# Keys, queries and values of dilated attention groups projected in class order: a strided stationary operand in a two-layer mixer on one core

## The chip, the core and the metric

The kernel runs on one core of a Trainium2 chip. The metric is device time in microseconds (us). TensorE (PE in the profile, its weight loads PEld), VectorE (DVE), ScalarE (ACT) and GpSimd (POOL) run in parallel, each with its own instruction stream; SyncE (SP) issues most DMAs.

## The reference, cut to what matters

Two decoder layers over 512 tokens and 1024 features. In each layer one normed input is projected for four attention branches, A to D. Branch B has three groups of 8 heads; group 0 attends to neighbouring tokens, group 1 to every 4th, group 2 to every 16th.

```python
B_GROUPS = ((128, 1), (512, 4), (2048, 16))      # window, dilation
xn = rms_norm(x, norm_gain[l])
qbm = rms_norm(b_q.reshape(shp_b), qk_gain_b[l, 0])
kbm = rms_norm(b_k.reshape(shp_b), qk_gain_b[l, 1])
yb = dilated_mixture(qbm, kbm, b_v.reshape(shp_b), rel_bias)
...
def to_sub(t):    # keys and queries of one residue class stand together
    t = t.reshape(b, sub_len, dil, h, dh).transpose(0, 2, 1, 3, 4).reshape(b * dil, sub_len, h, dh)
```

## The kernel before

The normed residual is held feature-major, `xhl` [128 partitions, 2 parts, 8 row tiles, 512 tokens], as two exact fp32r parts (high and low). Every product of two such operands takes three passes: high by high, high by low, low by high. A weight slot is loaded by an SP DMA (`next_slot`, L402), its high part is made on ACT (L405) and its low part on DVE (L411); six split slots are kept.

A job `("pair", branch, p, g)` projects q, k and v of two heads: 384 columns, four slots. `t_bank` fills one PSUM bank per tile of 128 tokens: the stationary operand is the residual (128 tokens), the moving one the weights, 8 row tiles by 3 passes = 24 matmuls (L512 to L514). `f_bank` is the other orientation: weights stationary, all 512 tokens moving, 24 matmuls (L536 to L538). There are four such accumulating banks (`acc`).

Groups 1 and 2 of branch B (`perm` in `do_pair`) need their tokens in class order: token 4i + c at place 128c + i. So 4 pairs of heads x 2 groups x 2 layers = 16 jobs are permuted. For these, before the change: the four calls of `t_bank` make q and k alone (256 columns) in natural order; after the norms (`norm_qk`: square, sum, power, gain, split over ACT, DVE and POOL), PE transposes each head to feature-major (L676, L689) and the ACT copies out of PSUM (`q_out` L680, `k_out` L693) write with a permuting pattern; the unpermuted jobs use L682 and L696 instead. v is made by `f_bank`, copied by ACT in class order (L734), transposed back on PE in four 128x128 pieces (L737), and split into its two parts by one ACT and one DVE instruction of 512 columns (`split_ps`, L547, L548). For other jobs v lies in columns 256 to 384 of each `t_bank` and is split out of it, 128 columns at a time. `k_swap` copies k with high and low exchanged by four POOL DMAs (L701, L702). Attention of a class (`attend`, L971 to L1026) and the copy back to natural order (`o_sum`, L1041) take class order as input in both versions.

Each engine's instruction order is made by a scheduler from the list `PLAN`: earlier pieces are preferred, later ones (gates z, the merges of finished branches, the next pair) fill in where they are ready. It also places the tiles in SBUF.

Of the kernel before, what the change touches and what calls it, by code (L numbers as in the profile page):

```python
# [82 lines left out]
def job_slots(job):  # L83
    """Per weight slot: a list of (source, rows of 128, columns)."""
    kind = job[0]
    if kind in ("idx", "cin", "pair", "d0", "d1"):
        c = chunk_cols(job)
        return [[("w_in", 2 * i + j, c) for j in range(2)] for i in range(4)]
    if kind == "z":
        c = Z_OFF[job[1]] + job[2] * 128 + np.arange(128)  # L90
        return [[("w_in", 4 * i + j, c) for j in range(4)] for i in range(2)]
    if kind == "merge":
        n, ft = job[1], job[2]
        c = OFF_G + n * D + ft * 128 + np.arange(128)
        f = ft * 128 + np.arange(128)
        return [[("w_in", j, c) for j in range(6)],
                [("w_in", j, c) for j in (6, 7)] + [(("w_branch", n), j, f) for j in range(4)]]
    if kind == "out":
        f = job[1] * 128 + np.arange(128)
        return [[("w_out", 4 * i + j, f) for j in range(4)] for i in range(2)]  # L100
    if kind == "cq":
        q = job[1] * 384 + np.arange(384)
        return [[("w_q_b", 0, q), ("w_q_b", 1, q)]]
    if kind == "ckv":
        p = job[1]
        h = np.arange(64)
        kv = np.concatenate([(2 * p) * 128 + h, (2 * p + 1) * 128 + h,
                             (2 * p) * 128 + 64 + h, (2 * p + 1) * 128 + 64 + h])
        return [[("w_kv_b", 0, kv)]]
    raise ValueError(kind)  # L110


def plan():
    """The order of a layer's work; what comes first is preferred where several pieces are ready."""
# [127 lines left out]
def build(ctx, tc, A, depth=2, dump=None):  # L242
# [97 lines left out]
    def make_skew(seg, r):  # L340
        """Rows r and r + 1 of a segment, 128 copies each, so that a load can shift copy i by i."""
        r0, nr = (C_ROW, 1) if seg == "C" else (SEG_ROWS[seg][0] + r, 2)
        o = SEG_A if seg == "C" else seg
        w = SEG_W[o]
        d = dp.tile([nr, 128, w], F32, name=f"skew{seg}_{r}")
        g = gdram[r0:r0 + nr, o:o + w]
        sy.dma_start(d, bass.AP(tensor=g.tensor, offset=g.offset, ap=[[SEG_LEN, nr], [0, 128], [1, w]]))
        for i in range(nr):
            skew[seg, r0 + i] = (d[i], w)
# [9 lines left out]
    def next_skew():  # L359
        """The next segment's copies, behind the weights requested so far."""  # L360
        if skews:
            with tc.issue_after(wdma[0].ins):
                make_skew(*skews.pop(0))

    def load_bias(row, seg, n):
        """[128, n] tile whose row i is the segment's row shifted by i to the right."""
        while (seg, row) not in skew:
            next_skew()
        b = T([128, 512], F32, "bias")[:, :n]
        g, w = skew[seg, row]  # L370
        with tc.issue_after(wdma[0].ins):
            sy.dma_start(b, bass.AP(tensor=g.tensor, offset=g.offset + 127, ap=[[w - 1, 128], [1, n]]))
        return b

    def rsqrt(eng, r, ss, n, scale, eps=EPS):
        """r = 1 / sqrt(ss * scale + eps) on [128, n]."""
# [5 lines left out]
    def layer(l, xt):  # L382
# [32 lines left out]
        def gain_parts():  # L415
            """x * gain as hi and lo per row tile: the first products need not wait for the norm."""
# [87 lines left out]
        def t_bank(slots, w, t, c0=0, c1=None, x=None):  # L504
            c1 = w if c1 is None else c1
# [3 lines left out]
            for kt in range(KT):  # L509
                h, lo = slots[kt // 2]  # L510
                a = (kt % 2) * w
                mm(o[:, :c1 - c0], x[kt][:, 0, ts], h[:, a + c0:a + c1], start=kt == 0, stop=False)  # L512
                mm(o[:, :c1 - c0], x[kt][:, 0, ts], lo[:, a + c0:a + c1], start=False, stop=False)  # L513
                mm(o[:, :c1 - c0], x[kt][:, 1, ts], h[:, a + c0:a + c1], start=False, stop=kt == KT - 1)  # L514
            return o

        def t_banks(slots, w, x):
            """Banks of all token tiles, filled together; x: hi and lo per row tile."""
# [12 lines left out]
        def f_bank(parts, mh, ml, w=S):  # L531
            """parts: (hi, lo) stationary views [128, 128] per row tile; moving operands mh, ml: [128, w] each."""
# [11 lines left out]
        def split_ps(hi, lo, src, scale=None):  # L544
            """hi + lo = src (* scale), src in PSUM."""
# [92 lines left out]
        def evac(o, n, scale=1.0):  # L638
            """A copy of a bank's first n columns, so that the bank is free before the norms are known."""
# [7 lines left out]
        def norm_qk(o, t, x, gi, scale=1.0):  # L647
            """o: two heads of q and of k in PSUM; hi and lo of the normed ones to x[:, t], [128, 4, 2, 64]."""
# [13 lines left out]

        def perm_view(x, perm):
            return x.rearrange("p (c i) -> p i c", c=4) if perm else x
# [4 lines left out]
        def q_out(uq, qx, hf, h0, n, perm):  # L669
            """Heads of qx [128, 2, n, 2, 64] (half hf of the tokens) to uq[:, h0:h0 + n], feature-major."""  # L670
            for i0 in range(0, n, 2):
# [6 lines left out]
                if perm:  # L678
                    dst = uq[:, h0 + i0:h0 + i0 + m].rearrange("p h (c i) -> p h i c", c=4)[:, :, hf * 64:hf * 64 + 64]
                    ac.copy(dst, src.rearrange("p h (i c) -> p h i c", c=4))  # L680
                else:
                    ac.copy(uq[:, h0 + i0:h0 + i0 + m, hf * 256:hf * 256 + 256], src)  # L682

        def k_out(kk, x, hf, perm):
            """The two k heads of x (half hf of the tokens), hi on top of lo, to kk(h, 0)."""
# [4 lines left out]
            for i in range(2):  # L690
                src = p[:, i * 256:(i + 1) * 256]
                if perm:
                    ac.copy(kk(i, 0).rearrange("p (c i) -> p i c", c=4)[:, hf * 64:hf * 64 + 64],  # L693
                            src.rearrange("p (i c) -> p i c", c=4))
                else:
                    ac.copy(kk(i, 0)[:, hf * 256:hf * 256 + 256], src)  # L696

        def k_swap(kk):
            """kk(h, 1): lo on top of hi."""
# [8 lines left out]
        def do_pair(job):  # L708
# [6 lines left out]
            for t in range(NT):  # L715
                if t % 2 == 0:
                    x = T([128, 2, 4, 2, 64], F32R, "qk")
                o = t_bank(slots, 384, t, 0, 256 if perm else 384)
                if not perm:
                    v = o[:, 256:384].rearrange("p (h d) -> p h d", h=2)  # L720
                    split_ps(vv[:, t, :, 0:64], vv[:, t, :, 64:128], v)
# [3 lines left out]
                if t % 2:  # L725
                    q_out(uq, x, t // 2, 0, 2, perm)
                    k_out(kk, x, t // 2, perm)
            k_swap(kk)
            if perm:
                o = f_bank([(slots[k // 2][0][:, (k % 2) * 384 + 256:(k % 2) * 384 + 384],  # L730
                             slots[k // 2][1][:, (k % 2) * 384 + 256:(k % 2) * 384 + 384]) for k in range(KT)],
                           xhs, xls)
                vp = T([128, 512], F32, "tmp")
                ac.copy(perm_view(vp, True), nat_view(o, True))  # L734
                p = ps_t()
                for t in range(NT):
                    pe.transpose(p[:, t * 128:(t + 1) * 128], vp[:, t * 128:(t + 1) * 128], idf)  # L737
                pv = p.rearrange("p (t h d) -> p t h d", t=NT, h=2)
                split_ps(vv[:, :, :, 0:64], vv[:, :, :, 64:128], pv)
            return uq, ks, vv  # L740

        def do_d():
# [4 lines left out]
            for t in range(NT):  # L747
# [7 lines left out]
                if t % 2:  # L755
                    q_out(uqs[0], x, t // 2, 0, 2, False)
                    k_out(kk, x, t // 2, False)
# [3 lines left out]
            for t in range(NT):  # L761
# [10 lines left out]
                for i in range(3):  # L772
# [5 lines left out]
                    if t % 2:  # L778
                        q_out(uqs[i + 1], qxs[i], t // 2, 0, 2, False)
# [3 lines left out]
        def do_cin():  # L783
# [23 lines left out]
            # rotary key, shared by the heads  # L807
# [24 lines left out]
        def do_cq(p, cT):  # L832
            """The normed and rotated queries of two pairs, [128, 2, 4, 96] per half of the tokens."""
# [73 lines left out]
        def scores(kind, step, qk, bias, nm, den, mask, sink, both):  # L907
            """exp of the scores less their maximum, sums to den, minus the maximum to nm."""
# [52 lines left out]
        def attend(kind, qk, v, bias, nm, den, norm, both, mask=None, sink=None):  # L961
            """qk(qb, k0, n): (lhsT, rhs) of the passes; v(kb): stationary [128, 128]; nm/den [128, NT] columns.
            Returns the O bank: rows of V's high part on top of rows of its low part."""
# [73 lines left out]
        def o_sum(dst, o, h, perm):  # L1037
            """Add the halves of an O bank into rows h*64.. of dst, in token order."""
# [290 lines left out]
```

## Time and profile before

| | us |
|---|---|
| median of 3 runs | 1953.87 |
| lowest, highest | 1952.23, 1957.49 |
| the profiled execution: its span, first to last instruction | 1949.2 |
| PE busy in it | 1884.5 (97%) |
| DVE busy | 1331.1 (68%) |
| ACT busy | 1103.0 (57%) |
| POOL busy | 728.5 (37%) |
| granted TensorE clock, mean | 0.986 of full |

For the profiled execution the profile gives the span; the median lies 4.7 us above it. "Busy" of PE counts overlapping matmul records once; how fast PE works is read from the distance between the starts of consecutive matmuls, not from their durations, since a matmul's record overlaps the next one's. PEld is PE's loading of a stationary operand, which runs beside the matmul of the one before it.

### The profile page before, as it was taken

How to read it: one execution, taken by the hardware profiler on the slowest of the kernel's cores; microseconds unless marked ns; L12 is line 12 of the kernel's file. 1: busy time of each engine (PE TensorE's matmuls, PEld its weight loads, DVE VectorE, ACT ScalarE, POOL GpSimd, SP SyncE). 2: the span in 40 equal slices, each digit the busy share in tenths (PEclk: the TensorE clock that was granted, in tenths of full speed). 3: DMA queues.
4: the chain of work that ended last, by engine and by line, in shares of the span. 5: the costliest groups of instructions: out<-in, count | busy, mean ns of one | idle time of the engine just before them, and what ended most of it. 6: DMA issues, size and time to landing. Idle time of an engine off the chain costs nothing.

```text
span 1949.2 us, 33221 instructions
## 1 busy us (share of the span) xinstructions
PE 1884.5 (97%) x11348; PEld 1695.6 (87%) x11348; DVE 1331.1 (68%) x3410; ACT 1103.0 (57%) x2650; POOL 728.5 (37%) x1186
## 2 busy tenths in 40 slices
PE   8759999999989999999999999999999999999999
PEld 7648889989878998998889988899899989898887
DVE  7649777758476866665469888676768686766542
ACT  6538666656455565554347776566555656555431
POOL 3615353424233346640005345253343343755000
PEclk9879999999989999999999999999999999999999
DMA  4223233342334243332252222233333333333233
GB/s 163 84 91 95 67 90 103 105 113 88 110 105 118 80 121 105 99 98 82 91 187 85 82 66 93 74 88 83 94 105 113 101 101 91 117 96 101 80 92 108
DMA packets 103420, 193.47 MB, mean 99 GB/s; under 512 B 21510, under 2 KB 35924, under 8 KB 103252
## 3 DMA queue, kind: packets, MB, share of 16 engines
q1 hardware_dynamic: 92372, 173.52, 29.4%
q0 software_dynamic: 10880, 17.83, 4.2%
q8 instruction: 90, 1.47, 0.3%
q14 instruction: 78, 0.64, 0.1%
HBM read 168.84 MB, written 12.83 MB: 93 GB/s over the span
## 4 chain that ended last, share of the span: by engine, by line
PE 88%; DMA 4%; DVE 2%; ACT 2%; POOL 2%; issue 1%; SPq 1%; DVEq 0%; ACTq 0%; POOLq 0%
PE acc L537 14%; PE acc L536 14%; PE acc L538 14%; PE acc L512 9%; PE acc L513 9%; PE acc L514 9%; PE S L923 4%; PE T L994 3%; PE T L1014 2%; DMA cbuf<-wall 1%; DMA sd<-st 1%; PE T L1033 1%; PE T L1026 1%; PE T L676 1%; PE T L689 1%
## 5 line engine op out<-in xcount | busy, mean ns | idle before, releaser
L411 DVE TENSOR_TENSOR cbufr<-cbuf,cbufr 128x768 fp32r<-128x768 f32 (+3 forms) x396 | 357.6, 906 | 140.5 <-ACT cbufr L405 139.0
L405 ACT CAST cbufr<-cbuf 128x768 fp32r<-128x768 f32 (+3 forms) x396 | 304.9, 774 | 262.4 <-PE acc L537 195.9
L513 PE MATMUL acc<-cbufr 128*128 128x384 f32 (+1 forms) x1152 | 365.8, 318 | 0.0
L512 PE MATMUL acc<-cbufr 128*128 128x384 f32 (+1 forms) x1152 | 364.1, 317 | 0.0
L514 PE MATMUL acc<-cbufr 128*128 128x384 f32 (+1 forms) x1152 | 363.9, 316 | 0.0
L536 PE MATMUL acc<-cbufr 128*128 128x512 f32 x896 | 354.5, 396 | 0.9 <-ACT raw L642 0.9
L538 PE MATMUL acc<-cbufr 128*128 128x512 f32 x896 | 353.9, 395 | 0.0
L537 PE MATMUL acc<-cbufr 128*128 128x512 f32 x896 | 353.6, 395 | 0.0
L513 PEld LDWEIGHTS acc<-cbufr 128*128 128x128 f32 x1152 | 218.7, 190 | 3.0 <-issue 1.1
L512 PEld LDWEIGHTS acc<-cbufr 128*128 128x128 f32 x1152 | 218.5, 190 | 2.7 <-ACT U L696 0.7
L514 PEld LDWEIGHTS acc<-cbufr 128*128 128x128 f32 x1152 | 218.7, 190 | 2.3 <-issue 0.8
L379 POOL TENSOR_TENSOR nr<-nx,cbuf 128x4 f32<-128x4 f32 (+2 forms) x200 | 211.6, 1060 | 11.1
L538 PEld LDWEIGHTS acc<-cbufr 128*128 128x128 f32 x896 | 168.9, 188 | 34.0
L536 PEld LDWEIGHTS acc<-cbufr 128*128 128x128 f32 x896 | 169.0, 189 | 32.7 <-ACT raw L642 1.3
L537 PEld LDWEIGHTS acc<-cbufr 128*128 128x128 f32 x896 | 169.1, 189 | 32.3 <-issue 0.7
L958 POOL TENSOR_SCALAR P<-P,rd 128x128 f32<-128x128 f32 x192 | 117.3, 621 | 195.4 <-DVE rd L956 136.2
L378 POOL TENSOR_SCALAR nx<-nss 128x4 f32<-128x4 f32 (+2 forms) x200 | 62.3, 311 | 272.2 <-DVE nss L653 243.1
L701 POOL DMA_DIRECT2D U<-U x68 | 39.3, 578 | 311.4 <-ACT U L693 190.4
L547 ACT CAST PT<-T 128x128 fp32r<-128x128 f32 (+2 forms) x224 | 102.9, 478 | 64.0 <-PE T L994 38.0
L548 DVE TENSOR_TENSOR PT<-T,PT 128x128 fp32r<-128x128 f32 (+2 forms) x224 | 119.8, 548 | 22.0 <-ACT PT L547 20.3
L945 ACT ACTIVATE P<-P,nm 128x128 f32<-128x128 f32 x192 | 101.9, 533 | 57.4 <-DVE nm L942 56.7
L642 ACT COPY raw<-acc 128x256 f32<-128x256 f32 (+2 forms) x192 | 70.4, 377 | 107.9 <-PE acc L514 74.9
(256 smaller groups left out, 3954.0 us busy)
## 6 DMA issues: line engine op xcount, KB each, us to landing
cbuf<-wall SPq DMA_DIRECT2D x284, 384.0 KB
cbuf<-wall SPq DMA_DIRECT2D x96, 256.0 KB
U<-U POOLq DMA_DIRECT2D x136, 128.0 KB, 2.8
bias<-skew SPq DMA_DIRECT2D x32, 128.0 KB
bias<-skew SPq DMA_DIRECT2D x16, 256.0 KB
skew<-gdram SPq DMA_DIRECT2D x8, 384.0 KB
cbuf<-wall SPq DMA_DIRECT2D x8, 328.0 KB
skew<-gdram SPq DMA_DIRECT2D x4, 640.0 KB
```

The source lines that it names most:

```text
L379: gp.tensor_tensor(r, y, mhalf[:, :n], op=OP.pow)
L405: pin(ac.copy(h, raw))
L411: pin(e.tensor_tensor(lo, raw, h, op=OP.subtract))
L512: mm(o[:, :c1 - c0], x[kt][:, 0, ts], h[:, a + c0:a + c1], start=kt == 0, stop=False)
L513: mm(o[:, :c1 - c0], x[kt][:, 0, ts], lo[:, a + c0:a + c1], start=False, stop=False)
L514: mm(o[:, :c1 - c0], x[kt][:, 1, ts], h[:, a + c0:a + c1], start=False, stop=kt == KT - 1)
L536: mm(o[:, :w], h, mh[kt], start=kt == 0, stop=False)
L537: mm(o[:, :w], h, ml[kt], start=False, stop=False)
L538: mm(o[:, :w], lo, mh[kt], start=False, stop=kt == n - 1)
L547: ac.copy(hi, src)
L548: ve.tensor_tensor(lo, src, hi, op=OP.subtract)
L958: gp.tensor_scalar(p[:, off:off + nk * 128], p[:, off:off + nk * 128], rd[:, qb:qb + 1], 0.0, op0=OP.mult, op1=OP.add)
```

## The change

The stationary operand of `t_bank` becomes, for permuted jobs, every fourth token of the residual (`xperm`: 128 elements of 4 bytes, 16 bytes apart), so that a bank holds one class, already in order. v goes into the same bank (384 columns, like the other jobs), and the permuting copies, `f_bank` for v, its class copy and its transposes go. The program is also built with `dynamic_dma_scratch_size=4096`, an argument that sets how much of SBUF is kept for the DMAs that POOL issues. Comments and docstrings are blanked (left out here).

```diff
-        def t_bank(slots, w, t, c0=0, c1=None, x=None):
-            c1 = w if c1 is None else c1
+        def t_bank(slots, w, t, x=None, perm=False):
+
             x = x or [xhl[:, :, kt] for kt in range(KT)]
             o = ps_acc()
             ts = slice(t * 128, (t + 1) * 128)
             for kt in range(KT):
                 h, lo = slots[kt // 2]
                 a = (kt % 2) * w
-                mm(o[:, :c1 - c0], x[kt][:, 0, ts], h[:, a + c0:a + c1], start=kt == 0, stop=False)
-                mm(o[:, :c1 - c0], x[kt][:, 0, ts], lo[:, a + c0:a + c1], start=False, stop=False)
-                mm(o[:, :c1 - c0], x[kt][:, 1, ts], h[:, a + c0:a + c1], start=False, stop=kt == KT - 1)
+                xs = [xperm[kt][:, e, t] if perm else x[kt][:, e, ts] for e in range(2)]
+                mm(o[:, :w], xs[0], h[:, a:a + w], start=kt == 0, stop=False)
+                mm(o[:, :w], xs[0], lo[:, a:a + w], start=False, stop=False)
+                mm(o[:, :w], xs[1], h[:, a:a + w], start=False, stop=kt == KT - 1)
             return o
...
+        xperm = [xhl[:, :, kt].rearrange("p e (i c) -> p e c i", c=4) for kt in range(KT)]
+
...
-        def q_out(uq, qx, hf, h0, n, perm):
-            """Heads of qx [128, 2, n, 2, 64] (half hf of the tokens) to uq[:, h0:h0 + n], feature-major."""
+        def q_out(uq, qx, hf, h0, n):
+
...
-                if perm:
-                    dst = uq[:, h0 + i0:h0 + i0 + m].rearrange("p h (c i) -> p h i c", c=4)[:, :, hf * 64:hf * 64 + 64]
-                    ac.copy(dst, src.rearrange("p h (i c) -> p h i c", c=4))
-                else:
-                    ac.copy(uq[:, h0 + i0:h0 + i0 + m, hf * 256:hf * 256 + 256], src)
...
+                ac.copy(uq[:, h0 + i0:h0 + i0 + m, hf * 256:hf * 256 + 256], src)
...
-                if perm:
-                    ac.copy(kk(i, 0).rearrange("p (c i) -> p i c", c=4)[:, hf * 64:hf * 64 + 64],
-                            src.rearrange("p (i c) -> p i c", c=4))
-                else:
-                    ac.copy(kk(i, 0)[:, hf * 256:hf * 256 + 256], src)
+                ac.copy(kk(i, 0)[:, hf * 256:hf * 256 + 256], src)
...
-                o = t_bank(slots, 384, t, 0, 256 if perm else 384)
-                if not perm:
-                    v = o[:, 256:384].rearrange("p (h d) -> p h d", h=2)
-                    split_ps(vv[:, t, :, 0:64], vv[:, t, :, 64:128], v)
+                o = t_bank(slots, 384, t, perm=perm)
+                v = o[:, 256:384].rearrange("p (h d) -> p h d", h=2)
+                split_ps(vv[:, t, :, 0:64], vv[:, t, :, 64:128], v)
                 last = norm_qk(o, t % 2, x, int(br == BR_B))
...
             k_swap(kk)
-            if perm:
-                o = f_bank([(slots[k // 2][0][:, (k % 2) * 384 + 256:(k % 2) * 384 + 384],
-                             slots[k // 2][1][:, (k % 2) * 384 + 256:(k % 2) * 384 + 384]) for k in range(KT)],
-                           xhs, xls)
-                vp = T([128, 512], F32, "tmp")
-                ac.copy(perm_view(vp, True), nat_view(o, True))
-                p = ps_t()
-                for t in range(NT):
-                    pe.transpose(p[:, t * 128:(t + 1) * 128], vp[:, t * 128:(t + 1) * 128], idf)
-                pv = p.rearrange("p (t h d) -> p t h d", t=NT, h=2)
-                split_ps(vv[:, :, :, 0:64], vv[:, :, :, 64:128], pv)
             return uq, ks, vv
...
-    nc = bacc.Bacc("TRN2", target_bir_lowering=False, num_devices=1)
+    nc = bacc.Bacc("TRN2", target_bir_lowering=False, num_devices=1, dynamic_dma_scratch_size=4096)
```

## Rows read from the trace of the kernel before

**Rows 1.** The page, busy us of each engine (share of the span), instructions.

```profile
PE 1884.5 (97%) x11348; PEld 1695.6 (87%) x11348; DVE 1331.1 (68%) x3410; ACT 1103.0 (57%) x2650; POOL 728.5 (37%) x1186
```

**Rows 2.** Windows: us; PE, PEld, DVE, ACT, POOL busy (instructions); clock, DMA share, GB/s.

```profile
330.00:560.00 230.00, 213.91 (x1435) 196.33 (x1434) 146.78 (x411) 126.07 (x297) 79.87 (x136) 0.96 0.39 108
...
1330.00:1660.00 330.00, 330.00 (x2172) 301.87 (x2171) 240.22 (x648) 200.49 (x471) 122.12 (x197) 1.00 0.36 101
```

**Rows 3.** Waits of PE, 330 to 560 us: total us, times, longest.

```profile
PE T L1026 <- DVE PT L548: 12.3, 3, 5.2
...
PE T L1026 <- ACT PT L547: 3.4, 1, 3.4
```

**Rows 4.** Waits of PE, 560 us to the end.

```profile
PE S L923 <- DMA U<-U: 1.3, 1, 1.3
```

**Rows 5.** Groups on PE by form: count, busy us, mean ns, idle before.

```profile
L536 PE MATMUL acc<-cbufr 128*128 128x512 f32 x896 | 354.5, 396 | 0.9 <-ACT raw L642 0.9
...
L512 PE MATMUL acc<-cbufr 128*128 128x256 f32 x512 | 145.7, 285 | 0.0
...
L737 PE MATMUL T<-cbuf,tmp 128*128 128x128 f32 x64 | 9.6, 272 | 0.0
```

**Rows 6.** Timeline of PE: start us, us; 256 columns, a permuted pair.

```profile
339.78 0.28 PE L513 MATMUL acc<-cbufr 128*128 128x256 f32 x1
...
340.98 0.28 PE L514 MATMUL acc<-cbufr 128*128 128x256 f32 x1
```

**Rows 7.** Timeline of PE: 384 columns, an unpermuted pair.

```profile
612.33 0.33 PE L514 MATMUL acc<-cbufr 128*128 128x384 f32 x1
...
614.23 0.33 PE L513 MATMUL acc<-cbufr 128*128 128x384 f32 x1
```

**Rows 8.** Timeline of PE: 512 columns in f_bank.

```profile
584.68 0.39 PE L538 MATMUL acc<-cbufr 128*128 128x512 f32 x1
...
588.08 0.39 PE L538 MATMUL acc<-cbufr 128*128 128x512 f32 x1
```

**Rows 9.** Timeline of PE: the transposes of v and what follows.

```profile
368.32 0.60 PE L737 MATMUL T<-cbuf,tmp 128*128 128x128 f32 x4
368.68 0.37 PE L514 MATMUL acc<-cbufr 128*128 128x256 f32 x1
368.88 0.28 PE L512 MATMUL acc<-cbufr 128*128 128x256 f32 x1
```

**Rows 10.** Timeline of PEld: five weight loads on end, for narrow score matmuls.

```profile
157.95 0.64 PEld L923 LDWEIGHTS S<-U,U 128*128 128x128 f32 x5
```

**Rows 11.** Groups on ACT by form: permuting copies and plain ones.

```profile
L693 ACT CAST U<-T 128x256 fp32r<-128x256 f32 x64 | 36.2, 673 | 2.4 <-PE T L689 2.3
L680 ACT CAST U<-T 128x512 fp32r<-128x512 f32 x32 | 35.5, 1111 | 21.8 <-PE T L676 21.6
...
L682 ACT CAST U<-T 128x512 fp32r<-128x512 f32 x48 | 28.1, 599 | 3.4 <-PE T L676 3.2
...
L696 ACT CAST U<-T 128x256 fp32r<-128x256 f32 x72 | 23.9, 393 | 9.3 <-PE T L689 8.5 <-ACT th L1051 0.7
L547 ACT CAST U<-acc 128x128 fp32r<-128x128 f32 x96 | 23.6, 271 | 27.9 <-PE acc L514 26.5 <-PE acc L873 0.7
...
L734 ACT COPY tmp<-acc 128x512 f32<-128x512 f32 x16 | 17.7, 1104 | 0.1
```

**Rows 12.** Groups on ACT by form: copies out of PSUM, plain and permuted reading.

```profile
L1043 ACT COPY tmp<-T 64x512 f32<-64x512 f32 x64 | 37.2, 581 | 30.1 <-PE T L1014 21.5 <-PE T L1033 7.4
...
L1041 ACT COPY G<-T 64x512 f32<-64x512 f32 x32 | 18.5, 578 | 36.6 <-PE T L1026 35.7
```

**Rows 13.** Groups on DVE by form: splits of v.

```profile
L548 DVE TENSOR_TENSOR U<-acc,U 128x128 fp32r<-128x128 f32 x96 | 25.0, 280 | 13.9 <-ACT U L547 13.9
```

**Rows 14.** DMA issues: KB each, us from issue to landing.

```profile
U<-U POOLq DMA_DIRECT2D x136, 128.0 KB, 2.8
```

More of the change, by code (lines that the diff above doesn't have):

```diff
@@ L677, in q_out, with k_out @@
                 src = p[:, :m * 256].rearrange("p (h s) -> p h s", h=m)
-                if perm:
-                    dst = uq[:, h0 + i0:h0 + i0 + m].rearrange("p h (c i) -> p h i c", c=4)[:, :, hf * 64:hf * 64 + 64]
-                    ac.copy(dst, src.rearrange("p h (i c) -> p h i c", c=4))
-                else:
-                    ac.copy(uq[:, h0 + i0:h0 + i0 + m, hf * 256:hf * 256 + 256], src)
-        def k_out(kk, x, hf, perm):
+                ac.copy(uq[:, h0 + i0:h0 + i0 + m, hf * 256:hf * 256 + 256], src)
+        def k_out(kk, x, hf):
             p = ps_t(F32R)
@@ L725, in do_pair @@
                 if t % 2:
-                    q_out(uq, x, t // 2, 0, 2, perm)
-                    k_out(kk, x, t // 2, perm)
+                    q_out(uq, x, t // 2, 0, 2)
+                    k_out(kk, x, t // 2)
             k_swap(kk)
-            if perm:
-                o = f_bank([(slots[k // 2][0][:, (k % 2) * 384 + 256:(k % 2) * 384 + 384],
-                             slots[k // 2][1][:, (k % 2) * 384 + 256:(k % 2) * 384 + 384]) for k in range(KT)],
-                           xhs, xls)
-                vp = T([128, 512], F32, "tmp")
-                ac.copy(perm_view(vp, True), nat_view(o, True))
-                p = ps_t()
-                for t in range(NT):
-                    pe.transpose(p[:, t * 128:(t + 1) * 128], vp[:, t * 128:(t + 1) * 128], idf)
-                pv = p.rearrange("p (t h d) -> p t h d", t=NT, h=2)
-                split_ps(vv[:, :, :, 0:64], vv[:, :, :, 64:128], pv)
             return uq, ks, vv
@@ L755, in do_d @@
                 if t % 2:
-                    q_out(uqs[0], x, t // 2, 0, 2, False)
-                    k_out(kk, x, t // 2, False)
+                    q_out(uqs[0], x, t // 2, 0, 2)
+                    k_out(kk, x, t // 2)
             k_swap(kk)
@@ L778, in do_d @@
                     if t % 2:
-                        q_out(uqs[i + 1], qxs[i], t // 2, 0, 2, False)
+                        q_out(uqs[i + 1], qxs[i], t // 2, 0, 2)
             return uqs, ks, vv
```

## The prediction

> **What bounds the kernel now.** I read four views, in this order. The page first: PE is busy 97% of the span and no other engine above 68% [rows 1]. Then the windows by stage, since a mean hides stages: in the second layer's branch B (1330 to 1660 us) PE has not one idle microsecond, while in the first layer's (330 to 560) it lacks 16.1 us and the clock is 0.96 [rows 2]. Then PE's waits: in that early stretch they are class attention (L1026) waiting for DVE and ACT [rows 3]; after 560 us the largest is one of 1.3 us for k's swap [rows 4]. So from 560 us on, what PE spends is the time, one for one; work saved on ACT, DVE or POOL saves nothing by itself. Last, PE's own pace. The durations of [rows 5] can't be added up, since records overlap (285 ns for a matmul that starts 120 ns after its neighbour); the distance between starts can:
>
> - 256 columns: ten steps from 339.78 to 340.98, 0.120 us each [rows 6].
> - 384 columns: eleven steps from 612.33 to 614.23, 0.173 us [rows 7].
> - 512 columns: fifteen steps from 584.68 to 588.08, 0.227 us [rows 8].
> - A weight load of 128 columns, where the matmuls are too short to hide it: five loads in 0.64 us, the last one itself 0.19, so (0.64 - 0.19) / 4 = 0.112 us from load to load [rows 10].
>
> A matmul's pace is thus the longer of its columns and the next load. At 384 columns the load has 0.173 - 0.112 = 0.061 us to spare, and nobody sees it.
>
> **The matmuls.** One permuted job loses the 24 matmuls of 512 columns (24 x 0.227 = 5.45 us) and four transposes: from 368.32 to 368.88, less the one 256-column step inside, 0.44 us [rows 9]. The transposes number 64 in 16 jobs [rows 5], four per job. Its 96 matmuls of 256 columns become 96 of 384: 96 x (0.173 - 0.120) = 5.09 us more. The columns streamed are equal (96 x 256 + 24 x 512 = 96 x 384); what goes is the fixed part of 24 matmuls, and the transposes. Net 5.45 + 0.44 - 5.09 = 0.80 us per job, 12.8 us in 16 jobs. This is the whole direct gain: 0.7%.
>
> **The weight loads, which now read every fourth token.** 96 x 16 = 1536 loads read 128 elements 16 bytes apart. No stationary or moving operand of the kernel before has such a pattern, so the trace has no price and I bound it. Below: nothing, as ACT's copy out of PSUM with a permuted reading pattern takes 578 ns against 581 for the plain one [rows 12]. Above: ACT's permuted copies into SBUF. The same cast of 128x512 takes 1111 instead of 599 ns, a factor of 1.86; by slope, (1111 - 673) / 256 = 1.71 ns per element against (599 - 393) / 256 = 0.80, a factor of 2.13 [rows 11]. On a load of 0.112 us these factors give 0.208 and 0.238 us, both over the 0.173 that hides it, and the load then sets the pace. Which row is nearer? The one without a price reads PSUM; those with one touch SBUF with one element per place, as the new load does, though writing. I take SBUF's side, and of it 1.93, between the whole-instruction factor and twice: 0.216 us. That is 0.216 - 0.173 = 0.043 us on 1536 matmuls, 66 us. Bounds: 0 and (0.238 - 0.173) x 1536 = 100 us. Nothing covers it, since PE has no idle time there [rows 2]; in the first layer's stretch with 16.1 us of idleness some of it may vanish, a few us at most.
>
> What the Trainium skill says stands beside this. Its page "SBUF — State Buffer", section "Specifications (TRN2)", names lines of 16 bytes, at least two hits per line for full bandwidth, and a penalty for each crossing. It gives no figure; a load with one hit per line falls under it, and if the penalty is a doubling, as on ACT, the load would be 0.224 us and the sum 66 us larger by 0.008 x 1536 = 12 us. No run so far shows it on a load.
>
> **ACT, DVE, POOL.** ACT loses 16 copies of 1104 ns (17.7 us), 32 x (1111 - 599) = 16.4 us and 64 x (673 - 393) = 17.9 us; it gains 64 splits of 271 ns (17.3 us) less the 16 wide ones they replace [rows 11]. DVE gains at most 64 x 280 ns = 17.9 us [rows 13]. Both I cost at nothing: PE covers them, at 57% and 68% busy. Were that cover gone, ACT's saving of some 35 us would be the gain. A bank is now held until ACT and DVE have split v, some 0.55 us longer (271 + 280 ns); with four banks of 24 x 0.173 = 4.2 us, that is hidden. Queued behind these splits is `norm_qk` of the same bank, and the swap of k waits for its chain.
>
> **What f_bank covered.** From a job's last bank until k's swap has landed runs a chain over all engines, of which the swap alone has 2.8 us from issue to landing [rows 14]; PE filled it with 5.9 us of v. Now attention of the job must be covered by gates, merges and the next pair. Unpermuted jobs have no `f_bank` either, and after 560 us PE loses 1.3 us once to such a swap [rows 4]. I take nothing; upper bound 16 x 1.3 = 21 us.
>
> **The POOL argument.** It leaves the packer more room in SBUF and POOL's DMAs less. They come in fours (136 in 34 jobs) of 128 KB [rows 14], a k swap per job, far apart. I take nothing; if each of the four had to wait for its forerunner to land, a swap would take 3 x 2.8 = 8.4 us longer, mostly under other work.
>
> **Sum.** Against the profiled execution's 1949.2 us: -12.8 + 66 = +53. The median lies 4.7 us above that span, outside the stages touched, and moves along: 1953.87 + 53 = 2007.
>
> **Rivals.** The second one ends on the other side.
>
> 1. The strided load sets the pace (forecast): 2007, between 1954 - 12.8 + 54 = 1995 (factor 1.86) and 1954 - 12.8 + 100 = 2041 (2.13). For it: the ACT rows, and that a load is a read of SBUF at one element per place. Against it: no strided read in the trace is slower. Chance 0.52.
> 2. The strided load stays under 0.173 us and only PE's saving is left: 1954 - 12.8 = 1941. For it: [rows 12], and 0.061 us of slack, so that a load may grow by a factor of 1.54. That is the point from which it decides: each further 0.001 us costs 1.5 us, and at 0.181 us, a factor of 1.62, the gain is used up. Chance 0.34. The skill's page "TensorE: Matmul & The Clock Gate", section "LDWEIGHTS (loading the stationary operand)", counts a load's columns alone, at about 107 ns for 128, which [rows 10] bears out with 112, and names no stride there; by that section alone this rival would be the outcome.
> 3. The load stays hidden, but the gain goes into waits: attention waits for the swap that `f_bank` covered, or the early stretch's waits [rows 3], which hang on DVE's order, grow. 0.5 to 1.3 us per job, 8 to 21 us: 1949 to 1962, about no change. For it: PE waits on L1026 already. Against: [rows 4]. Chance 0.10.
> 4. Each of the 128 elements costs a fetch of its own, as long as four neighbours together: the load 4 x 0.112 = 0.448 us, (0.448 - 0.173) x 1536 = 422 us, so 2360. Nothing in the rows is slowed by four. Chance 0.04.
>
> **Chances and range.** A measurement here can tell about 0.3% (6 us) from no change. Rival 2 lies 13 us below, with the new order of the scheduler worth some 5 us either way: nearly all of its 0.34 is faster, 0.03 of it same. Rival 3 gives 0.06 same and 0.04 slower. Rivals 1 and 4 are slower. Together: faster 0.31, same 0.09, slower 0.60. The forecast's own range is 1995 to 2041; as rival 2 holds more than 2 in 10, the range reaches to it with its 5 us: 1936 to 2041.
>
> **What the profile after would show.** The matmuls of `t_bank` for permuted jobs at 384 columns with starts 0.21 to 0.22 us apart (forecast) or 0.173 (rival 2); their weight loads recorded longer than 0.19 us; PE's groups for 256 columns in L512 to L514, L734 and L737 gone; L680's and L693's permuted forms replaced by 599 and 393 ns; ACT's busy time some 35 us less and the end unmoved by it; PE's waits after 560 us still a few us (if they reach 10 or more, rival 3). The prediction is wrong if the starts of those matmuls lie under 0.18 us apart.

## The result and the profile after

| | us |
|---|---|
| before, median of 4 runs beside the changed kernel | 1953.14 |
| after, median of 4 runs (lowest, highest) | 2040.92 (2040.02, 2041.89) |
| ratio after to before, 95% interval | 1.0443 [1.0428, 1.0458] |
| span of the profiled execution, before and after | 1949.2 and 2040.1 |

The changed kernel is slower by 87.8 us. The page gives the busy time of each engine, as [rows 1] does for the kernel before:

```profile
PE 1976.0 (97%) x10900; PEld 1802.1 (88%) x10900; DVE 1349.0 (66%) x3458; ACT 1065.6 (52%) x2682; POOL 731.2 (36%) x1186
```

PE has 448 instructions fewer (16 jobs of 24 matmuls and 4 transposes) and is busy 91.5 us longer; the span is longer by 90.9. ACT lost 37.4 us and the end didn't move with it. The windows of the two stretches of branch B, in the columns of [rows 2] (the second layer's now lies from 1390 to 1730):

```profile
330.00:590.00 260.00, 243.65 (x1300) 229.09 (x1299) 149.11 (x420) 116.80 (x307) 83.53 (x133) 0.97 0.36 96
1390.00:1730.00 340.00, 339.67 (x1849) 318.88 (x1849) 232.12 (x642) 169.35 (x454) 119.50 (x189) 1.00 0.34 92
```

In the second layer PE is as full as before, at a granted clock of 1.00 (2.4 GHz); the clock is not the cause. PE lacks 16.3 us in the first layer's stretch, against 16.1 before, and its waits there are the same two (class attention, now L1009), as in [rows 3]:

```profile
PE T L1009 <- ACT PT L548: 12.2, 2, 9.5
PE T L1009 <- DVE PT L549: 4.1, 2, 3.7
```

From 590 us to the end all of PE's waits come to 1.2 us; the wait for k's swap of [rows 4] is gone:

```profile
PE acc L513 <- DVE s L1120: 0.7, 2, 0.3
PE acc L537 <- ACT raw L643: 0.5, 1, 0.5
```

So no wait took the time. What did is seen in the groups on PE (the columns of [rows 5]) and on PEld. `t_bank` is now L513 to L515, `f_bank` L537 to L539:

```profile
L514 PE MATMUL acc<-cbufr 128*128 128x384 f32 x1152 | 428.2, 372 | 0.0
...
L537 PE MATMUL acc<-cbufr 128*128 128x512 f32 x768 | 303.3, 395 | 0.9 <-ACT raw L643 0.9
```

```profile
L513 PEld LDWEIGHTS acc<-cbufr 128*128 128x128 f32 x1152 | 289.2, 251 | 3.8 <-DVE s L1120 1.4 <-issue 0.5
...
L537 PEld LDWEIGHTS acc<-cbufr 128*128 128x128 f32 x768 | 144.9, 189 | 28.7 <-ACT raw L643 1.3
```

Each of the three lines of `t_bank` has 1152 loads, 512 of them from the 16 permuted jobs. Their mean is 251 ns where `f_bank`'s plain loads have 189. Taking 188 ns for the other 640, the strided ones last (1152 x 251 - 640 x 188) / 512 = 330 ns. The timelines of PE and of PEld in a permuted job (the pair of [rows 6], which stood at 0.120 us) show it singly:

```profile
341.22 0.39 PE L515 MATMUL acc<-cbufr 128*128 128x384 f32 x1
...
345.42 0.40 PE L515 MATMUL acc<-cbufr 128*128 128x384 f32 x1
```

```profile
341.26 0.33 PEld L513 LDWEIGHTS acc<-cbufr 128*128 128x128 f32 x1
...
342.90 0.33 PEld L514 LDWEIGHTS acc<-cbufr 128*128 128x128 f32 x1
```

PE makes eighteen steps in 4.20 us, 0.233 us each; PEld seven steps in 1.64 us, 0.234 us each, with records of 0.33 us. Matmul and load go in step at a pace that 384 columns alone don't have (0.173 in [rows 7]). On ACT the permuting copies of [rows 11] have become plain ones (L681, 593 ns; L691, 388 ns), with 64 more splits of v in the row of L548:

```profile
L681 ACT CAST U<-T 128x512 fp32r<-128x512 f32 x80 | 46.8, 593 | 38.4 <-PE T L679 38.3
L691 ACT CAST U<-T 128x256 fp32r<-128x256 f32 x136 | 44.8, 388 | 28.5 <-PE T L688 25.7 <-DMA gdram<-th 2.6
L548 ACT CAST U<-acc 128x128 fp32r<-128x128 f32 x160 | 41.1, 275 | 104.4 <-PE acc L515 103.1 <-PE acc L856 0.7
```

### The profile page after: what moved, and what is told of

Same layout as the page of the kernel before. It is cut to its first block, busy times and chain, and to the rows that moved or that the text cites. A ratio compares the mean times of both kernels' runs of the same rounds, so it can differ in the third digit from the quotient of the medians.

```text
span 2040.1 us, 32284 instructions
## 1 busy us (share of the span) xinstructions
PE 1976.0 (97%) x10900; PEld 1802.1 (88%) x10900; DVE 1349.0 (66%) x3458; ACT 1065.6 (52%) x2682; POOL 731.2 (36%) x1186
## 4 chain that ended last, share of the span: by engine, by line
PE 91%; DMA 3%; DVE 2%; SPq 2%; ACT 1%; issue 1%; POOL 0%; ACTq 0%; DVEq 0%; POOLq 0%
PE acc L539 13%; PE acc L538 13%; PE acc L537 13%; PE acc L514 12%; PE acc L513 12%; PE acc L515 12%; PE S L906 4%; PE T L977 3%; PE T L997 2%; DMA cbuf<-wall 1%; PE T L1016 1%; PE T L1009 1%; PE T L679 1%; DMA gdram<-th 1%; PE T L688 1%; DMA sd<-st 1%
## 5 line engine op out<-in xcount | busy, mean ns | idle before, releaser
L405 ACT CAST cbufr<-cbuf 128x768 fp32r<-128x768 f32 (+3 forms) x396 | 306.6, 778 | 255.8 <-PE acc L538 174.1
L514 PE MATMUL acc<-cbufr 128*128 128x384 f32 x1152 | 428.2, 372 | 0.0
L513 PE MATMUL acc<-cbufr 128*128 128x384 f32 x1152 | 426.3, 370 | 0.7 <-DVE s L1120 0.7
L515 PE MATMUL acc<-cbufr 128*128 128x384 f32 x1152 | 426.6, 370 | 0.0
L537 PE MATMUL acc<-cbufr 128*128 128x512 f32 x768 | 303.3, 395 | 0.9 <-ACT raw L643 0.9
L538 PE MATMUL acc<-cbufr 128*128 128x512 f32 x768 | 303.3, 395 | 0.0
L539 PE MATMUL acc<-cbufr 128*128 128x512 f32 x768 | 303.3, 395 | 0.0
L514 PEld LDWEIGHTS acc<-cbufr 128*128 128x128 f32 x1152 | 289.1, 251 | 5.1 <-issue 3.6
L513 PEld LDWEIGHTS acc<-cbufr 128*128 128x128 f32 x1152 | 289.2, 251 | 3.8 <-DVE s L1120 1.4
L515 PEld LDWEIGHTS acc<-cbufr 128*128 128x128 f32 x1152 | 289.6, 251 | 2.5 <-issue 0.8
L379 POOL TENSOR_TENSOR nr<-nx,cbuf 128x4 f32<-128x4 f32 (+2 forms) x200 | 217.0, 1088 | 10.9
L537 PEld LDWEIGHTS acc<-cbufr 128*128 128x128 f32 x768 | 144.9, 189 | 28.7 <-ACT raw L643 1.3
L539 PEld LDWEIGHTS acc<-cbufr 128*128 128x128 f32 x768 | 144.8, 189 | 28.8
L538 PEld LDWEIGHTS acc<-cbufr 128*128 128x128 f32 x768 | 145.0, 189 | 27.4
L548 ACT CAST PT<-T 128x128 fp32r<-128x128 f32 (+2 forms) x224 | 103.5, 478 | 102.8 <-PE T L977 86.1
L977 PE MATMUL T<-cbuf,P 128*128 128x128 f32 x672 | 117.0, 274 | 0.0
```

The lines of the kernel that those rows point to most:

```text
L379: gp.tensor_tensor(r, y, mhalf[:, :n], op=OP.pow)
L405: pin(ac.copy(h, raw))
L513: mm(o[:, :w], xs[0], h[:, a:a + w], start=kt == 0, stop=False)
L514: mm(o[:, :w], xs[0], lo[:, a:a + w], start=False, stop=False)
L515: mm(o[:, :w], xs[1], h[:, a:a + w], start=False, stop=kt == KT - 1)
L537: mm(o[:, :w], h, mh[kt], start=kt == 0, stop=False)
```

## The experiments

The theory: each of the 1536 strided loads lasts longer than its neighbour's 384 columns can hide, and that is the whole loss. The rivals for the loss: the wider matmuls themselves, the cover that `f_bank` gave, the smaller DMA scratch. Ratios are against the kernel before, run on the same chip in the same series.

**The stationary operand unstrided.** The changed kernel, but the permuted jobs read 128 neighbouring tokens; the dilated heads get the wrong tokens, and only the time is read.

```diff
-                xs = [xperm[kt][:, e, t] if perm else x[kt][:, e, ts] for e in range(2)]
+                xs = [x[kt][:, e, ts] for e in range(2)]
```

> The changed kernel, but the stationary operand of the permuted jobs is 128 neighbouring tokens instead of every fourth, so that those heads are computed from tokens in natural order; all else is as changed. Load theory: the matmuls of the permuted jobs start 0.173 us apart instead of 0.233, their loads are recorded with 0.19 us, and the time falls by 1536 x 0.060 = 92 us and a few more, to 1941 (1933 to 1949), some 12 us under the kernel before. Rival, lost cover (attention waits for what f_bank used to cover, or the new order costs): the time stays above 1960 and PE shows waits of over 20 us more than the kernel before. Rival, wider matmuls: 384 columns are slow in these jobs whatever their stationary operand, and the starts stay 0.2 us apart or more.

Measured: 1945.23 us (1944.43 to 1945.73), ratio 0.9959 [0.9946, 0.9973]. The timeline of PE in the same pair, twenty steps in 3.46 us, 0.173 us each:

```profile
339.37 0.33 PE L513 MATMUL acc<-cbufr 128*128 128x384 f32 x1
...
342.83 0.33 PE L515 MATMUL acc<-cbufr 128*128 128x384 f32 x1
```

The waits of PE from 330 to 590 us in this run:

```profile
PE T L1009 <- ACT PT L548: 13.9, 2, 11.5
PE T L1009 <- DVE PT L549: 5.2, 2, 4.7
```

With everything of the change kept but the stride, 95.7 us go (the kernel before had 1953.1 us in both series), and the kernel is 0.4% faster than before. The wider matmuls, the lost cover and the scratch are refuted as causes of the loss; the waits are even 2.8 us larger here than with the stride.

**Every second token (8 bytes apart).**

```diff
-                xs = [xperm[kt][:, e, t] if perm else x[kt][:, e, ts] for e in range(2)]
+                xs = [xhl[:, e, kt, min(t, 2) * 128:min(t, 2) * 128 + 256:2] if perm else x[kt][:, e, ts] for e in range(2)]
```

> The changed kernel with every second token as the stationary operand of the permuted jobs (8 bytes from one element to the next, two elements in 16 bytes; the wrong tokens, same work). If two elements in each 16 bytes are enough for full pace: loads recorded with 0.19 us, starts 0.173 us apart, time as with neighbouring tokens. If a load grows with the 16-byte stretches that it touches (64 instead of 32, where the change has 128): recorded 0.19 + (0.33 - 0.19) x 32 / 96 = 0.235 us, pace 0.152, still under 0.173, so the same time but longer records. If any step costs the whole doubling: 0.33 us records, starts 0.233 us apart, time near 2041.

Measured: 1945.93 us, ratio 0.9964 [0.995, 0.9979]. The group on PEld:

```profile
L514 PEld LDWEIGHTS acc<-cbufr 128*128 128x128 f32 x1152 | 221.1, 192 | 5.5 <-issue 3.6
```

By the sum used above, the strided 512 last (1152 x 192 - 640 x 188) / 512 = 197 ns, 9 more than plain ones. The timeline of PE shows twenty steps in 3.47 us, 0.173 us each:

```profile
340.50 0.34 PE L515 MATMUL acc<-cbufr 128*128 128x384 f32 x1
...
343.97 0.34 PE L514 MATMUL acc<-cbufr 128*128 128x384 f32 x1
```

The first of the three expectations came true: with two elements in each 16 bytes the load stays hidden. Skipping elements alone costs no time here.

**Every third token (12 bytes) and every eighth (32 bytes).** As the one above with a step of 3 and, across two row tiles, of 8 (other tokens than the reference's in both):

```diff
+                xs = [xhl[:, e, kt, min(t, 1) * 128:min(t, 1) * 128 + 384:3] if perm else x[kt][:, e, ts] for e in range(2)]
...
+                xs = [xhl[:, e].rearrange("p k s -> p (k s)")[:, min(kt, 6) * 512 + t:min(kt, 6) * 512 + 1024:8] if perm else x[kt][:, e, ts] for e in range(2)]
```

> As the run before with every third token (12 bytes apart, 96 stretches of 16 bytes touched). Growth with the stretches touched: records of 0.28 us, pace 0.193, 31 us slower than with neighbouring tokens, near 1972. A threshold at 16 bytes: as with neighbouring tokens, 0.19 us. Any step costs the doubling: 0.33 us and near 2041.

> As the run before with a step of eight elements (32 bytes apart, 128 stretches of 16 bytes touched, as in the change; data from two neighbouring row tiles, the wrong numbers, same work). If the cost is one access per 16-byte stretch, it is the change's: records of 0.33 us, starts 0.233 us apart, 2041. If it grows on with the distance: records of 0.4 us and more, and a time over 2100.

Measured: 1959.51 us, ratio 1.0033 [1.0018, 1.0047], for the step of 3; 2053.88 us, ratio 1.0515 [1.0496, 1.0535], for the step of 8. The timelines of PE, first the step of 3 (seventeen steps in 3.03 us, 0.178 us each), then the step of 8 (fifteen in 3.66 us, 0.244 us each):

```profile
339.92 0.34 PE L513 MATMUL acc<-cbufr 128*128 128x384 f32 x1
...
342.95 0.34 PE L515 MATMUL acc<-cbufr 128*128 128x384 f32 x1
```

```profile
340.24 0.41 PE L515 MATMUL acc<-cbufr 128*128 128x384 f32 x1
...
343.90 0.40 PE L515 MATMUL acc<-cbufr 128*128 128x384 f32 x1
```

The groups on PEld, first the step of 3, then the step of 8:

```profile
L514 PEld LDWEIGHTS acc<-cbufr 128*128 128x128 f32 x1152 | 251.9, 219 | 5.1 <-issue 3.6
```

```profile
L514 PEld LDWEIGHTS acc<-cbufr 128*128 128x128 f32 x1152 | 294.0, 255 | 5.1 <-issue 3.6
```

By the same sum the strided loads last 258 and 339 ns, where the step of 2 has 197 and the change 330. So at 12 bytes the load is already longer, but just at the edge of what 384 columns hide; none of the three times expected for it (1972, 1945, 2041) came out. From 16 to 32 bytes, twice the distance, the step grows only from 0.233 to 0.244 us and the time by 13 us: not quite the same time, as the first expectation had it, and far from the 2100 of the second. The price rises between 8 and 16 bytes and hardly any further up to 32, the longest step tried.

**The kernel before with the strided load.** q and k alone, 256 columns, are made in class order; nothing else of the change (the evictions still permute, so the tokens end in the wrong places).

```diff
-                mm(o[:, :c1 - c0], x[kt][:, 0, ts], h[:, a + c0:a + c1], start=kt == 0, stop=False)
...
+                xs = [xhl[:, e, kt].rearrange("p (i c) -> p c i", c=4)[:, t] if c1 - c0 < w else x[kt][:, e, ts] for e in range(2)]
+                mm(o[:, :c1 - c0], xs[0], h[:, a + c0:a + c1], start=kt == 0, stop=False)
```

> The kernel before, with one edit: the stationary operand of its permuted jobs' 256-column matmuls is every fourth token (so those heads are permuted twice: the wrong tokens, same work). Load theory: the load of 0.233 us sets the pace whatever the columns, so 0.233 instead of 0.120 us, 1536 x 0.113 = 174 us: 1953 + 174 = 2127, up to 2140 with what short neighbours fail to hide. Rival, a strided operand adds a fixed 0.060 us to its matmul: 0.180 us, 92 us, 2045.

Measured: 2123.74 us, ratio 1.0878 [1.0854, 1.0902]. The timeline of PE, with 53 steps in 12.37 us, 0.233 us each, where [rows 6] has 0.120:

```profile
340.50 0.40 PE L515 MATMUL acc<-cbufr 128*128 128x256 f32 x1
...
352.87 0.40 PE L514 MATMUL acc<-cbufr 128*128 128x256 f32 x1
```

256 and 384 columns have the same pace with this load. A fixed addition of 0.060 us to each matmul is refuted (it would give 0.180 us and 2045): the load alone sets the pace, and (0.233 - 0.120) x 1536 = 174 us accounts for the 171 measured.

**The changed kernel with 512 moving columns** in the permuted jobs (wider products, of which the surplus is never used):

```diff
-                mm(o[:, :w], xs[0], h[:, a:a + w], start=kt == 0, stop=False)
...
+                n = 512 if perm else w
+                a = (kt % 2) * (768 - n)
+                mm(o[:, :n], xs[0], h[:, a:a + n], start=kt == 0, stop=False)
```

> The changed kernel with 512 moving columns instead of 384 in the permuted jobs (128 further columns of the same weight slot, whose results nobody reads), with every fourth token as before. Load theory: 512 columns take 0.227 us, still under the load's 0.233, so a third more columns are free: 2041 within 8 us. Rival, a fixed 0.060 us on each matmul with a strided operand: 0.227 + 0.060 = 0.287, 1536 x 0.054 = 83 us more, 2124.

Measured: 2056.56 us, ratio 1.0534 [1.0513, 1.0555]. The timeline of PE, eighteen steps in 4.23 us, 0.235 us each:

```profile
484.69 0.40 PE L516 MATMUL acc<-cbufr 128*128 128x512 f32 x1
...
488.92 0.39 PE L516 MATMUL acc<-cbufr 128*128 128x512 f32 x1
```

A third more columns cost 16 us instead of the 83 that the difference of 0.054 us between [rows 8] and [rows 7] would make on 1536 matmuls: the columns are now what is hidden. In the profiled executions (spans 2055.2 and 2040.1 us) PE is busy 10.9 us longer than in the changed kernel and idle 4.2 us longer. Why the steps grow by these few ns was not traced.

**A strided moving operand.** The run with neighbouring tokens, and the gates' `f_bank` (768 matmuls of 512 columns) streams the residual in class order (so the gates' tokens are in the wrong places).

```diff
+                       [v.rearrange("p (i c) -> p c i", c=4) for v in xhs], [v.rearrange("p (i c) -> p c i", c=4) for v in xls])
```

> The run with neighbouring tokens as stationary operand (1945), and the 32 gate jobs z with a permuted moving operand: 512 tokens in class order, each 16 bytes from the next (the gates then belong to other tokens; same work). 768 matmuls. If the moving side pays like the loads, twice the time per element: 0.227 to 0.45 us, 768 x 0.22 = 171 us, 2116. If it pays the same 0.95 ns per element as a load did (0.233 - 0.112 over 128): 512 x 0.95 = 0.49 us more each, 373 us, 2318. If the moving side reads any pattern at full pace: 1945.

Measured: 2108.66 us in one run. The timeline of PE, eight steps in 3.69 us, 0.461 us each, where [rows 8] has 0.227:

```profile
668.03 0.64 PE L538 MATMUL acc<-cbufr 128*128 128x512 f32 x1
...
671.72 0.65 PE L537 MATMUL acc<-cbufr 128*128 128x512 f32 x1
```

The moving operand pays as well, by a factor of 2.03. By this one run, the change could not have got class order for nothing by turning the product around.

**The kernel before with the scratch argument alone.**

```diff
-    nc = bacc.Bacc("TRN2", target_bir_lowering=False, num_devices=1)
+    nc = bacc.Bacc("TRN2", target_bir_lowering=False, num_devices=1, dynamic_dma_scratch_size=4096)
```

> The kernel before with the new program argument for POOL's DMAs alone. As predicted, nothing: 1953 within 6 us, swaps of k landing in 2.8 us. Rival, POOL's DMAs wait for room: POOL's issues longer than 0.6 us, swaps later by up to 8.4 us, and a time over 1960.

Measured: 1952.02 us over 10 runs, ratio 0.9993 [0.9983, 1.0003]: no effect. The swaps of k still land in 2.8 us.

**A version meant to beat both.** The run with neighbouring tokens shows 8 us to be had from v in the bank of q and k. The kernel before permutes q and k in its evictions at no price to PE; here v alone takes another way, by DRAM, and ends in class order too. The scratch argument is that of the change.

```diff
+            vd = dp.tile([512, 2, 128], F32R, name=f"vd{uid[0]}") if perm else None
...
-                o = t_bank(slots, 384, t, 0, 256 if perm else 384)
...
+                o = t_bank(slots, 384, t)
+                v = o[:, 256:384].rearrange("p (h d) -> p h d", h=2)
+                if perm:
+                    vn = T([128, 512], F32R, "bm")[:, :256].rearrange("p (h d) -> p h d", h=2)
+                    split_ps(vn[:, :, 0:64], vn[:, :, 64:128], v)
+                    gp.dma_start(vd[t * 128:(t + 1) * 128], vn)
...
-                o = f_bank([(slots[k // 2][0][:, (k % 2) * 384 + 256:(k % 2) * 384 + 384],
...
+                gp.dma_start(vv, vd.rearrange("(p c) h d -> p c h d", c=4))
```

> This kernel is the one before with only v changed: v is projected in the bank of q and k (384 columns, residual read in token order, neighbouring columns as stationary operand), its two parts are written in token order, stored to DRAM by one DMA for each token tile (128 KB) and read back in class order by one DMA for each pair (512 KB, 4 KB for each partition: token 4p + c lies in partition p), both issued by GpSimd. q and k take class order in the evictions, as before; the bank of v alone, its eviction and its four transposes are gone. Load theory (the whole loss of the changed kernel is its strided stationary operand): TensorE does what it does with neighbouring tokens, so 1945 us (1941 to 1950), ratio 0.996, starts of the 384-column matmuls 0.173 us apart. Rival (the way by DRAM is late): the products with v wait for two DMAs in a row, 2.8 us each by the row of 136 DMAs before the change, up to 16 x 5.6 = 90 us if none of it is covered, or GpSimd's queue waits for the stores and holds up the norms; then 1953 us or more, and TensorE's waits show a DMA as the releaser at the class attention's products.

> As the kernel with v by DMA, but the read back in class order is issued by SP's queue, which also issues the loads of the weights; GpSimd issues the stores only. If GpSimd's queue is what loses time in the other kernel (its wait for the stores stands ahead of the norms), this one is faster than that by the 16 waits of 2 to 3 us, up to 40 us; if the way by DRAM is hidden in both, the two agree within 3 us at 1945 us (1941 to 1950). If SP's wait delays the weights, TensorE's waits show the split of the weights or a DMA as releaser, and the time is above the other's.

> The kernel with v by DMA, without the DMAs: q and k take class order in the evictions, v stays in token order (so the products of the dilated heads take the wrong rows of v; only the time is read). The kernel with v by DMA took 1976.3 us where the load theory alone gave 1945. If the way by DRAM is what cost those 31 us, this one takes 1945 us (1941 to 1950). If it is ACT's permuting evictions in the new order (ACT has 16.4 + 17.9 us more to do than in the run with neighbouring tokens), it takes 1960 us or more.

> The kernel with v by DMA, all of its DMAs issued by SP's queue, so that GpSimd issues no more than in the kernel before. If GpSimd's queue, where the stores wait for DVE's splits ahead of the norms, costs the 31 us, this takes 1945 to 1955 us, unless SP's waits hold up the weights. If it is the landing of v, or the order that follows from it, it stays at 1965 to 1980 us, as with the read alone on SP (1979.0).

Measured: 1976.3 us, ratio 1.0119 [1.0102, 1.0137], with GpSimd issuing; 1979.0 us, 1.0136 [1.0116, 1.0156], with the read back on SP; 1982.01 us, 1.0151 [1.0133, 1.0168], with all of it on SP; 1948.01 us, 0.9976 [0.9967, 0.9984], without these DMAs. So the way by DRAM costs 28 to 34 us, whichever queue issues it, and ACT's permuting evictions at most 3 (1948.01 against the 1945.23 of the run with neighbouring tokens). All three versions that keep v right are slower than the kernel before. The windows from 330 to 740 us, without the DMAs and with them (GpSimd issuing), say where most of the loss is:

```profile
330.00:740.00 410.00, 390.99 (x2376) 363.97 (x2375) 286.02 (x784) 227.90 (x573) 163.43 (x250) 0.98 0.39 107
```

```profile
330.00:740.00 410.00, 382.10 (x2279) 352.54 (x2278) 275.56 (x750) 212.67 (x546) 162.94 (x278) 0.96 0.43 120
```

PE idles 9 us more in this stretch of the first layer, its granted clock there is 0.96 instead of 0.98, and 97 matmuls fewer are done in it. None of PE's large waits names these DMAs. The largest wait that the kernel without them doesn't have is at 542 us, in the timelines of ACT and of PE:

```profile
540.69 0.83 ACT L405 CAST cbufr<-cbuf 128x768 fp32r<-128x768 f32 x1 [12.16 <-DMA cbuf<-wall]
```

```profile
541.97 0.86 PE L990 MATMUL T<-cbuf,P 128*128 128x128 f32 x2 [7.55 <-ACT P L977]
```

ACT stands for 12.16 us at the split of a weight slot whose DMA has not landed; the exponentials of attention (L977) are queued behind it, and PE waits 7.55 us for those. The idle time is paid twice: while PE stands idle the granted clock goes to 0.50 (1.2 GHz), and the window from 542 to 546 us, with PE at work again, is still at 0.50.

```profile
538.00:540.00 2.00, 0.00 (x0) 0.00 (x0) 0.00 (x0) 0.00 (x0) 0.00 (x0) 0.50 0.13 51
542.00:546.00 4.00, 4.00 (x14) 3.67 (x15) 4.00 (x15) 3.14 (x13) 0.00 (x0) 0.50 0.13 52
550.00:552.00 2.00, 2.00 (x19) 1.90 (x18) 0.25 (x1) 0.59 (x1) 0.00 (x0) 1.00 0.69 223
```

That is one wait. ACT's waits at L405 for weights, in all of the kernel (us in total, times), without the DMAs, with GpSimd issuing and with all of them on SP:

```profile
  DMA cbuf<-wall: 46.6, 11
  DMA cbuf<-wall: 57.8, 17
  DMA cbuf<-wall: 47.0, 11
```

With all DMAs on SP the weights are waited for no longer than without them, and the time is the longest of all: late weights are not the cause that the three versions share. Whether the order that the scheduler makes around v's later arrival is, these runs do not show; it stays open.

## Why the prediction was right, point by point

**Right: the load sets the pace.** The forecast was 2007 us, the measurement 2040.92: slower, as forecast, but 34 us above it and only just within the range, which ends at 2041. That the range held is in part luck: its end combines a saving of 12.8 us and a stride of 100, both some 5 us too large by the runs (7.9 and 95.7). Matmul and load in step, the unstrided run and the equal pace of 256, 384 and, nearly, 512 columns show the mechanism as it was put: the longer of columns and next load.

**Mis-sized: the price of the load, 66 us.** The term took a factor of 1.93, halfway between the 1.86 of ACT's whole permuting writes and twice, hence 0.216 us. Measured was 0.233 us, above the 0.21 to 0.22 expected, a factor of 0.233 / 0.112 = 2.08, hence (0.233 - 0.173) x 1536 = 92 us in long rows; over the whole kernel the stride costs 95.7 us. The upper bound of 0.238 us, from ACT's slope per element, was the nearer row. A reason can be given (like the slope, the pace of loads on end leaves out what an instruction takes besides its elements), but no run tests it, nor whether ACT's writes and PE's loads share a cause: that the one gave a fair price for the other was an analogy that held.

**Mis-sized: PE's saving, 12.8 us.** The unstrided run has 7.9 us of it (1953.09 to 1945.23). The distances from start to next start, added up by kind over the traces of the kernel before and of the unstrided run, with PE's idle time left out, say where it went: `f_bank` gives some 90 us (forecast 16 x 5.45 = 87.2) and the transposes 6 (7.0), but the banks of q and k take some 89 more (81.4), since in the mean of the kernel, with other work between them, 384 columns cost 0.181 us and 256 cost 0.123, 0.058 apart and not 0.053. The two errors add up: -7.9 + 95.7 = 87.8 against the forecast -12.8 + 66 = 53.

**Right: ACT, DVE and POOL at nothing.** ACT's busy time fell by 37.4 us and the time rose; DVE's rose by 17.9. That both lie so near the forecast is chance: its "some 35" leaves out the 16 wide splits that it names (16 x 604 ns = 9.7 us), with which the sum is 44, and DVE's splits of v take only 7.4 us more (43.4 against 25.0 + 11.0), the rest of the 17.9 lying in its other work. **Right: `f_bank`'s cover and the scratch at nothing.** PE's waits after 590 us are 1.2 us, and the scratch alone gives 0.9993.

**The rivals.** The hidden load fell, at 0.233 us against the 0.173 from which it decided; so did waits that eat the gain, and the four-fold fetch: at 32 bytes the pace is 2.18 times 0.112, not more.

The Trainium skill's page "SBUF — State Buffer", section "Specifications (TRN2)", asks for two hits per 16-byte line. The runs agree and add the size: with two of four elements read the load stays hidden under 0.173 us, its record 9 ns longer than a plain one's; with one it takes twice as long. An estimate from that page's line, by which each line touched costs two elements' time, would give 64, 96, 128 and 128 lines 1, 1.5, 2 and 2 times 0.112 us, that is 0.112, 0.168, 0.224 and 0.224, beside 0.173 (hidden), 0.178, 0.233 and 0.244 measured. It was made after the runs and comes out 4 to 8% short where the load shows; no run shows the inside of a line. The Trainium skill's page "TensorE: Matmul & The Clock Gate", section "LDWEIGHTS (loading the stationary operand)", counts columns alone; for 128 strided columns the measurement differs, 0.233 us, and decides.

## What to carry to other kernels

A weight load is free only while it is shorter than the matmul that runs over it: before a stationary operand gets a stride, compare twice the pace of loads on end with the pace of the matmuls (the factor of two is measured here for 4-byte elements 16 bytes apart or more). In this kernel the permutation was cheapest where an engine with idle time wrote it: ACT's permuting evictions, some 34 us more than plain ones, were hidden but for at most 3, and moving that work into TensorE's reads cost 96. Removing 0.4% of PE's work is easily given back: by the stride here, and by 28 us or more when v went through DRAM.

## What was not expected of the hardware

- The price of the stride rises up to 16 bytes and hardly after: nothing to be seen at 8 bytes (0.173 us, hidden), at the edge at 12 (0.178), 0.233 at 16, 0.244 at 32.
- At 16 bytes the moving operand pays too, 0.461 us instead of 0.227 for 512 columns in one run, while ACT's permuted reads out of PSUM cost nothing [rows 12].
- Under a load that sets the pace, 512 columns cost about what 256 do: 0.235 and 0.233 us.
